# First MLP product in seven block products, token sums beside the second product, and a residual kept in DRAM

## The chip, the cores and the metric

The program runs on one core of a Trainium2 chip. The metric is the device time of one execution in microseconds (us). A core has a matrix engine (TensorE, PE in the rows; its weight loads are PEld), a vector engine (VectorE, DVE), a scalar engine (ScalarE, ACT), GpSimd (POOL) and a queue that issues transfers (SyncE, SP). Each engine takes its own instructions in order; semaphores join them. Matrix products are summed in eight PSUM banks of 128 x 512 float32; everything else lies in SBUF, with 128 partitions.

## The reference, cut to what matters

Two layers of a hybrid backbone on 640 tokens (512 latent, 128 context), model width 1024. Layer 0 mixes by a recurrence and a Fourier transform, layer 1 by attention. What the change touches is the channel mixer at the end of each layer and its modulation:

```python
def ada_params(cond, w, b):
    m = jax.nn.silu(cond) @ w + b
    return jnp.split(m[..., None, :], 6, axis=-1)
...
def mlp(h, w1, b1, w2, b2):
    return jnp.square(jax.nn.relu(h @ w1 + b1)) @ w2 + b2
...
        xs = layer_norm(ALPHA * xs + ms[2] * ys, ln1_g[layer], ln1_b[layer])
        hs = modulate(xs, ms[3], ms[4])
        xs = layer_norm(ALPHA * xs + ms[5] * mlp(hs, w1[layer], b1[layer], w2[layer], b2[layer]),
                        ln2_g[layer], ln2_b[layer])
```

The context tokens go the same way with modulation vectors of their own. `w1` is 1024 x 4096, `w2` 4096 x 1024, all in float32.

## The kernel before, in words

**Products.** Every float32 operand is held as a high part `hi` and a low part `lo` (two float32r values that sum to it), and a product is three matmuls: weight hi by token hi, weight hi by token lo, weight lo by token hi. L210 issues nearly all of them.

**Weights.** Weights stream in units of 128 x 1024. SP loads a unit into one of three `raw` slots; `pump` (L163) takes it on: ACT copies the high part (L170), DVE subtracts it for the low part (L171), both into one of four `sp` slots. Two units are kept ready ahead. A `w1` unit holds 128 of the 4096 hidden columns, over all 1024 rows.

**The MLP** (`mlp`, L1026 on) goes through the hidden columns in four quarters b. In a quarter, eight `w1` units give 48 matmuls each (three products, eight row chunks, and the 640 tokens as 384 and 256 columns), 384 in all. A unit leaves PSUM through ACT (L1020, adds the bias), DVE (L1022, squared ReLU), ACT (L294, high part) and DVE (L297, low part) into `h1`. Then eight `w2` units, four for each half n of the output columns, give 240 matmuls of 512 columns (`tok_k_outer`): five token tiles of 128 stand in five banks at once, and after the fourth unit DVE multiplies each by the gate (L490) and POOL adds it into the residual `x` in SBUF (L493). The last quarter's second product is done tile by tile with the closing layer norm (`tail`).

**The first quarter** has extra work. The layer norm before it ends there: four `w1` units run early on the tokens that are ready (EARLY), while the last tiles are transposed. Then `make_base` scales `x` and adds gate times bias: POOL L504 for two products, DVE L506 for five tiles.

**Modulation of the next layer.** While layer 0's MLP runs, DVE works out the modulation vectors of layer 1 (`ada_sum_gen`): 48 steps, each with a 512 KB weight tile from DRAM and two passes of 128 x 1024 into `acc` (L428 the first, L430 after), one step for each weight unit that `next` hands out. After eight steps PE sums over the partitions, and DVE adds the bias (L455); gates go through a small DRAM buffer (`gscr`, POOL DMA L463).

**Slots.** `R` has 6 large tiles (tokens `hT` 2, `h1` 2, `x` and others), `vec` 4, `n` 6 of 128 x 1024, `acc` 1. A tile that asks for a slot waits for its last reader. The order on each engine is the program's order as a scheduler lays it out.

## Time and profile before

| | |
|---|---|
| Median of three runs | 1516.93 us (1514.2 to 1518.15) |
| The profiled execution | 1518.29 us, span of its trace 1516.2 us |
| Mean granted TensorE clock | 0.984 |
| PE / DVE / ACT / POOL busy | 1464.1 / 850.8 / 594.4 / 286.1 us |

The span is from the first to the last instruction; 2.1 us of the execution's time lie outside it. Busy times are sums over an engine's instructions. The layer-0 MLP runs from about 249 to 711 us and the layer-1 MLP from about 1058 us to the end.

### The profile page before, as it was taken

What the parts mean: (1) busy time and instruction counts of PE and PEld (TensorE: products, weight loads), DVE (VectorE), ACT (ScalarE), POOL (GpSimd) and SP (SyncE); (2) the same over time, 40 slices, a digit from 0 to 9 for tenths busy, and PEclk for the clock granted to TensorE, in tenths of its full rate; (3) what the DMA queues carried; (4) which work ended last, traced back from release to release, by engine and by line L of the source; (5) the groups of instructions that cost most, each with busy time, mean ns of one, the idle gap of its engine ahead of it and who ended that gap; (6) DMA issues with size and microseconds to landing.
All of it is one profiled execution on the core that took longest, in us unless ns stands there. A gap on an engine that the chain in (4) does not pass through costs nothing.

```text
span 1516.2 us, 21740 instructions
## 1 busy us (share of the span) xinstructions
PE 1464.1 (97%) x8572; PEld 1266.9 (84%) x8572; DVE 850.8 (56%) x1541; ACT 594.4 (39%) x1061; POOL 286.1 (19%) x327
## 2 busy tenths in 40 slices
PE   6999899999999999999899999999999999999997
PEld 4768677888988988988688888877998998988986
DVE  6756768974864865337744455547833333323345
ACT  4557436421321321336455455646531331321331
POOL 1145103104004004002412222322202103003000
PEclk9999999999999999999899999999999999999999
DMA  9445834453643642220533131431322222222211
GB/s 384 148 164 172 306 108 146 152 194 106 196 151 112 196 147 89 84 97 30 209 106 105 60 136 60 161 109 42 127 82 77 77 78 76 74 79 84 70 56 70
DMA packets 56373, 186.60 MB, mean 123 GB/s; under 512 B 10440, under 2 KB 10824, under 8 KB 56272
## 3 DMA queue, kind: packets, MB, share of 16 engines
q1 hardware_dynamic: 55440, 184.14, 35.3%
q8 instruction: 67, 1.10, 0.3%
q0 software_dynamic: 832, 1.09, 0.2%
q14 instruction: 34, 0.28, 0.1%
HBM read 178.87 MB, written 6.33 MB: 122 GB/s over the span
## 4 chain that ended last, share of the span: by engine, by line
PE 76%; DVE 11%; ACT 5%; issue 4%; POOL 2%; DMA 2%; SPq 0%; POOLq 0%; DVEq 0%; ACTq 0%
PE bank L210 74%; DVE sp L171 2%; PE bank L1212 1%; POOL ln L514 1%; ACT R L755 1%; DVE R L506 1%; DVE R L297 1%; DVE R L495 1%; ACT junk L512 1%; DVE R L526 1%; DVE ln L533 1%; DVE acc L430 1%; ACT n L567 1%; DVE n L524 1%; POOL n L1202 1%
## 5 line engine op out<-in xcount | busy, mean ns | idle before, releaser
L210 PE MATMUL bank<-R,sp 128*128 128x384 f32 (+1 forms) x4368 | 664.5, 311 | 10.7 <-POOL R L296 3.6
L210 PEld LDWEIGHTS bank<-R,sp 128*128 128x128 f32 x4368 | 642.7, 190 | 28.4 <-issue 7.5
L210 PE MATMUL bank<-sp,R 128*128 128x512 f32 x2580 | 613.4, 396 | 7.1 <-DVE sp L171 2.6
L210 PEld LDWEIGHTS bank<-sp,R 128*128 128x128 f32 x2580 | 484.2, 189 | 128.3 <-issue 8.2
L171 DVE TENSOR_TENSOR sp<-raw,sp 128x1024 fp32r<-128x1024 f32 (+1 forms) x177 | 219.1, 1240 | 171.5 <-ACT sp L170 166.8
L170 ACT ACTIVATE sp<-raw 128x1024 fp32r<-128x1024 f32 (+1 forms) x177 | 186.1, 1056 | 316.0 <-PE bank L210 299.0
L493 POOL TENSOR_TENSOR R<-R,n 128x512 f32<-128x512 f32 x60 | 91.0, 1551 | 499.8 <-DVE n L490 499.8
L1022 DVE SCALAR_TENSOR_TENSOR n<-n 128x640 f32<-128x640 f32 x64 | 52.6, 822 | 189.3 <-ACT n L1020 189.3
L1020 ACT ACTIVATE n<-bank,pack 128x384 f32<-128x384 f32 (+1 forms) x128 | 61.2, 524 | 234.0 <-PE bank L210 228.4
L430 DVE SCALAR_TENSOR_TENSOR acc<-n,cx,acc 128x1024 f32<-128x1024 f32 x84 | 110.5, 1352 | 7.4 <-DMA n<-in_ada_w_dram 7.4
L297 DVE TENSOR_TENSOR R<-n,R 128x640 fp32r<-128x640 f32 (+2 forms) x123 | 98.6, 805 | 14.1 <-POOL R L296 11.1
L490 DVE TENSOR_TENSOR n<-bank,vec 128x512 f32<-128x512 f32 x100 | 67.3, 685 | 40.7 <-PE bank L210 36.6
L294 ACT ACTIVATE R<-n 128x640 fp32r<-128x640 f32 (+1 forms) x88 | 61.6, 704 | 44.3 <-DVE n L1022 39.5
L514 POOL TENSOR_TENSOR ln<-ln,mhalf 128x1 f32<-128x1 f32 x35 | 20.1, 575 | 296.8 <-DVE ln L513 296.8
L512 ACT ACTIVATE junk<-R,ln 128x1024 bf16<-128x1024 f32 x35 | 40.3, 1151 | 84.7 <-DVE ln L522 60.2
L210 PE MATMUL bank<-R,R 128*128 128x512 f32 x240 | 62.5, 405 | 0.0
L1202 POOL TENSOR_SCALAR n<-n,mx 128x384 f32<-128x384 f32 (+1 forms) x80 | 43.1, 541 | 91.1 <-DVE mx L1199 46.8
L567 ACT ACTIVATE n<-bank,mod 128x128 f32<-128x128 f32 x120 | 45.3, 455 | 26.5 <-PE bank L560 26.5
L210 PEld LDWEIGHTS bank<-R,R 128*128 128x128 f32 x240 | 44.4, 188 | 11.0
L1216 ACT ACTIVATE n<-bank 128x384 f32<-128x384 f32 (+1 forms) x80 | 32.9, 448 | 49.8 <-PE bank L1212 43.4
L1187 DVE CUSTOM_DVE_ANT_0 n<-bank,vec 128x256 f32<-128x256 f32 (+3 forms) x128 | 40.4, 350 | 13.2 <-PE bank L210 8.9
L1192 ACT ACTIVATE n<-n,mx 128x384 f32<-128x384 f32 x64 | 38.8, 610 | 20.4 <-DVE mx L1190 16.9
(153 smaller groups left out, 923.7 us busy)
## 6 DMA issues: line engine op xcount, KB each, us to landing
raw<-in_wts_dram SPq DMA_DIRECT2D x184, 512.0 KB, 3.2
n<-in_ada_w_dram SPq DMA_DIRECT2D x80, 512.0 KB, 4.4
vec<-in_rpb_dram SPq DMA_DIRECT2D x16, 512.0 KB, 3.9
R<-in_ada_dram SPq DMA_DIRECT2D x15, 512.0 KB, 10.0
vec<-in_vecs_dram SPq DMA_DIRECT2D x13, 512.0 KB, 5.3
vec<-gscr SPq DMA_DIRECT2D x10, 512.0 KB, 4.8
R<-in_x_dram SPq DMA_DIRECT2D x5, 512.0 KB, 5.0
R<-in_xg_dram SPq DMA_DIRECT2D x5, 512.0 KB, 5.9
```

Of the source, the lines that this page charges most:

```text
L170: self.nc.scalar.activation(s.t[:, 0, :cols], r.t[:, :cols], AF.Copy)
L171: self.nc.vector.tensor_tensor(out=s.t[:, 1, :cols], in0=r.t[:, :cols], in1=s.t[:, 0, :cols].bitcast(F32), op=OP.subtract)
L210: self.nc.tensor.matmul(out, lhsT, rhs, start=start, stop=stop)
L294: self.nc.scalar.activation(hi, src, AF.Copy)
L297: (self.nc.vector if lo_eng == "dve" else self.nc.gpsimd).tensor_tensor(out=lo, in0=src, in1=hi.bitcast(F32), op=OP.subtract)
L430: nc.vector.scalar_tensor_tensor(acc.t[:, cond, :], w.t, f, acc.t[:, cond, :], op0=OP.mult, op1=OP.add)
L490: nc.vector.tensor_tensor(out=tmp.t[:, :512], in0=o.t, in1=gates[t // 4].t[:, c], op=OP.mult)
L493: nc.gpsimd.tensor_tensor(out=x[:, t, c], in0=x[:, t, c], in1=tmp.t[:, :512], op=OP.add)
L512: nc.scalar.activation(self.junk, src, AF.Square, bias=m[:, 2:3], accum_out=m[:, 4:5])
L567: nc.scalar.activation(dst, tr.t[:, j * 128:(j + 1) * 128], AF.Identity, bias=sh, scale=sc)
L1020: nc.scalar.activation(v[:, c0:c1], o.t[:, :c1 - c0], AF.Identity, bias=b)
L1202: nc.gpsimd.tensor_scalar(p.t[:, :n], p.t[:, :n], m[:, 5:6], 1.0, op0=OP.mult, op1=OP.mult)
```

## The change

**Pairs by block products.** In quarters b = 1 to 3, two `w1` units are done together (`w1_pair`). Two units are 256 hidden columns; the 1024 rows are halved (`hT[0]`, `hT[1]`), the 640 tokens are halved, and the 256 columns are halved by unit. The 2 x 2 x 2 block product that needs eight block products is done with seven (the Winograd form of Strassen's scheme). A block product (`block_mm`) is 12 matmuls of 320 columns into one bank, so that a pair has 84 matmuls. Three of the four pieces of weight go through sums: POOL makes four sums of 128 x 512 (L209 to L212) from the two raw units, and the pair is split in four pieces (`split_pair`): one raw unit, two sums of 1024 columns, half a raw unit, by ACT L174 and DVE L175. Three pieces are kept ready ahead. The blocks leave PSUM by one ACT copy and seven DVE operations of 128 x 320 (L1164 to L1187); squared ReLU is on ACT for the first unit and on DVE (L1155) for the second; the second unit's low part is made on POOL (L355).

**Token sums.** The tokens' sums and differences of blocks (`T12`, `T34`, two more `R` tiles with hi and lo) are made once for each layer by `token_sums`, during the second product of quarter 0: eight steps, each with POOL full values (L1105, 128 x 640), a DVE sum (L1117 to L1130), an ACT high part and a DVE low part (L355). In layer 0 a step goes with each of the eight units; in layer 1 two steps with each of the last four.

**Residual in DRAM.** `x`, after its scaling, is written to DRAM (`xsum`, ten pieces of 256 KB) and its `R` slot freed. DVE multiplies a tile of the second product by its gate (L1197), and a POOL DMA with accumulation adds it to its piece in DRAM (L1199, 60 in all). In the last quarter `x` is read back.

**Order.** In layer 0, the scaling now stands ahead of the modulation work, which makes no step in the early units, two for each of the last four units of quarter 0, and 1.5 or 2 for each unit of the second products, none in the pairs. The sixth part of the modulation (the MLP gate of layer 1) is moved to layer 1's own quarter 0; there the scaling follows when its gate has come back (`late_base`, behind the fourth unit of the second product).

```diff
+    def split_pair(self, s):
+        nc = self.nc
+        r = self.raws
+        if self.sub == 0:
+            r0, r1 = r[0].t, r[1].t
...
+            self.split_unit(s, r0, 1024)
+            nc.gpsimd.tensor_tensor(out=s1, in0=r1[:, :512], in1=r1[:, 512:], op=OP.add)
+            nc.gpsimd.tensor_tensor(out=s2, in0=s1, in1=r0[:, :512], op=OP.subtract)
+            nc.gpsimd.tensor_tensor(out=s3, in0=r0[:, :512], in1=r1[:, :512], op=OP.subtract)
+            nc.gpsimd.tensor_tensor(out=s4, in0=r0[:, 512:], in1=s2, op=OP.subtract)
+            r.pop(0).done()
+        elif self.sub < 3:
+            self.split_unit(s, self.sums[self.sub - 1].t, 1024)
...
+            self.split_unit(s, r[0].t[:, 512:], 512)
...
+    def token_sums(self, hT, sums):
...
+        for g in range(2):
+            fa, a = full(0, 1, g)
+            fb, t1 = full(0, 0, g)
+            nc.vector.tensor_tensor(out=t1, in0=a, in1=t1, op=OP.subtract)
+            put(0, 0, g, t1)
+            yield
...
+    def w1_pair(self, l, m, hT, sums, dst):
...
+        s = self.next_sub()
+        o, p = self.block_mm(s, 0, hT[0], 0)
+        nc.scalar.activation(t1, p, AF.Copy)
+        o.done()
+        o, p = self.block_mm(s, 512, hT[1], 0)
+        stt(c11, p, b[0], t1, op0=OP.add, op1=OP.add)
+        o.done()
+        s.done()
+        s = self.next_sub()
+        o, p = self.block_mm(s, 512, T12, H2)
+        tt(out=u2, in0=p, in1=t1, op=OP.add)
...
+    def evac_sum(self, o, t, n, gates):
...
+        nc.vector.tensor_tensor(out=tmp.t[:, :512], in0=o.t, in1=gates[t // 4].t[:, n * 512:(n + 1) * 512], op=OP.mult)
+        o.done()
+        nc.gpsimd.dma_start(out=self.xsum[t][n], in_=tmp.t[:, :512], accum_op=OP.add)
+        tmp.done()
...
+                if l == 0:
+                    load_base()
+                    base()
+                self.ada = self.ada_sum_gen(1, range(5) if l == 0 else (5,))
+                next(self.ada)
+                self.ada_rate = ADA_W1
...
+                if self.paired(("w1", l, b * 8 + m)):
+                    self.w1_pair(l, b * 8 + m, hT, sums, [h1[(m + i) // 4].t[:, (m + i) % 4] for i in range(2)])
...
+                def late_base():
+                    self.ada_flush()
+                    base()
+                    to_memory()
+                    self.side, self.side_steps = self.token_sums(hT, sums), 2
...
-                        self.evac_gated(outs[t], x.t, t, n, gates)
+                        self.evac_sum(outs[t], t, n, gates)
```

Three places show what this makes of the engines' order. The first is DVE in layer 0 around the end of the second product of quarter 0 (`bank_135` to `bank_139` before and `bank_135` on after are the five tiles of the second column half; `acc` is the modulation's sum). Before:

```order
L171 TENSOR_TENSOR sp_40_3120<-raw_42_2986,sp_40_3120 128x1024
L171 TENSOR_TENSOR sp_41_3159<-raw_43_3040,sp_41_3159 128x1024
L171 TENSOR_TENSOR sp_42_3225<-raw_44_3084,sp_42_3225 128x1024
L490 TENSOR_TENSOR n_123_3194<-bank_135_3042,vec_10_2429 128x512
L490 TENSOR_TENSOR n_124_3197<-bank_136_3049,vec_10_2429 128x512
```

After:

```order
L355 TENSOR_TENSOR R_21_2872<-n_129_3138,R_21_2872 128x2x320
L355 TENSOR_TENSOR R_22_2940<-n_132_3206,R_22_2940 128x2x320
L511 TENSOR_TENSOR n_130_3189<-bank_140_3192,n_130_3189 128x512
L482 TENSOR_SCALAR acc_3_3198<-n_125_3085,cx_118 128x1024
L483 TENSOR_SCALAR acc_3_3198<-n_125_3085,cx_118 128x1024
L175 TENSOR_TENSOR sp_41_3208<-vec_13_3149,sp_41_3208 128x1024
L486 SCALAR_TENSOR_TENSOR acc_3_3198<-n_128_3136,cx_118,acc_3_3198 128x1024 x2
L486 SCALAR_TENSOR_TENSOR acc_3_3198<-n_131_3201,cx_118,acc_3_3198 128x1024 x2
L528 TENSOR_SCALAR mod_122<-bank_141_3241 128x4 x4
L175 TENSOR_TENSOR sp_42_3265<-vec_14_3150,sp_42_3265 128x1024
L486 SCALAR_TENSOR_TENSOR acc_3_3198<-n_133_3252,cx_118,acc_3_3198 128x1024 x2
L1197 TENSOR_TENSOR n_136_3298<-bank_135_3099,vec_10_2417 128x512
```

The five tiles' evacuations stood right behind the weight splits; now the token sums, modulation passes and splits of sums stand in front of them.

The second is DVE in a pair of layer 0's quarter 3 (`raw` a unit as loaded, `vec` a POOL sum, `n` a work tile, `bank` a block product). Before, a unit of quarter 1:

```order
L1022 SCALAR_TENSOR_TENSOR n_132_3354<-n_132_3354 128x640
L171 TENSOR_TENSOR sp_45_3429<-raw_47_3228,sp_45_3429 128x1024
L297 TENSOR_TENSOR R_21_3209<-n_132_3354,R_21_3209 128x640
L430 SCALAR_TENSOR_TENSOR acc_3_3220<-n_135_3427,cx_108,acc_3_3220 128x1024 x2
```

After, a pair of units:

```order
L175 TENSOR_TENSOR sp_92_5161<-raw_76_5000,sp_92_5161 128x1024
L1169 TENSOR_TENSOR n_199_5127<-bank_225_5172,n_198_5126 128x320
L1172 TENSOR_TENSOR n_198_5126<-bank_226_5186,n_199_5127 128x320
L175 TENSOR_TENSOR sp_93_5200<-vec_31_5162,sp_93_5200 128x1024
L1176 SCALAR_TENSOR_TENSOR n_199_5127<-bank_227_5203,pack,n_199_5127 128x320
L1178 TENSOR_TENSOR n_199_5127<-bank_226_5186,n_199_5127 128x320
L1181 SCALAR_TENSOR_TENSOR n_198_5126<-bank_228_5218,pack,n_198_5126 128x320
L175 TENSOR_TENSOR sp_94_5232<-vec_32_5163,sp_94_5232 128x1024
L1187 TENSOR_TENSOR n_199_5127<-n_199_5127,bank_229_5239 128x320
L1155 SCALAR_TENSOR_TENSOR n_199_5127<-n_199_5127 128x640
L175 TENSOR_TENSOR sp_95_5258<-raw_77_5011,sp_95_5258 128x512
L355 TENSOR_TENSOR R_27_5124<-n_198_5126,R_27_5124 128x640
```

The block operations are those of the quarter's first pair, and the splits between them those of the second; in this stretch no modulation pass is left.

The third is POOL at the end of layer 0's second product. Before, the ten additions of a quarter stand alone:

```order
L493 TENSOR_TENSOR R_15_1734<-R_15_1734,n_118_3030 128x512
L493 TENSOR_TENSOR R_15_1734<-R_15_1734,n_123_3194 128x512
L493 TENSOR_TENSOR R_15_1734<-R_15_1734,n_124_3197 128x512
L493 TENSOR_TENSOR R_15_1734<-R_15_1734,n_125_3200 128x512
L493 TENSOR_TENSOR R_15_1734<-R_15_1734,n_126_3203 128x512
```

After, of quarter 2's end and quarter 3's first pairs:

```order
L209 TENSOR_TENSOR vec_31_5162<-raw_77_5011 128x512
L210 TENSOR_TENSOR vec_31_5162<-vec_31_5162,raw_76_5000 128x512
L211 TENSOR_TENSOR vec_32_5163<-raw_76_5000,raw_77_5011 128x512
L212 TENSOR_TENSOR vec_32_5163<-raw_76_5000,vec_31_5162 128x512
L1199 DMA xsum_1_66<-n_193_5109 128x512
L1199 DMA xsum_1_68<-n_194_5112 128x512
L1199 DMA xsum_1_70<-n_195_5115 128x512
L1199 DMA xsum_1_72<-n_196_5118 128x512
L1199 DMA xsum_1_74<-n_197_5121 128x512
L209 TENSOR_TENSOR vec_33_5292<-raw_79_5170 128x512
```

The sums of the quarter's second pair (`vec_31`, `vec_32`) stand ahead of the five accumulating transfers of the second column half, those of the third pair (`vec_33`) behind them.

## Rows read from the trace of the kernel before

**Rows 1.** The page: busy time, share and count of each engine, and the chain of work that ended last, by engine and by line.

```profile
PE 1464.1 (97%) x8572; PEld 1266.9 (84%) x8572; DVE 850.8 (56%) x1541; ACT 594.4 (39%) x1061; POOL 286.1 (19%) x327
...
PE 76%; DVE 11%; ACT 5%; issue 4%; POOL 2%; DMA 2%; SPq 0%; POOLq 0%; DVEq 0%; ACTq 0%
```

**Rows 2.** The same chain in order of time, four of its pieces: start us, us, what.

```profile
287.60 1.15 DVE sp L171
288.79 35.63 PE bank L210 x224
...
553.77 127.98 PE bank L210 x698
...
1077.90 421.16 PE bank L210 x2399
```

**Rows 3.** The engines' busy time by stage (us, with counts), the granted clock, DMA share, GB/s: the first quarter's first and second product and the second quarter's first product in layer 0, the third quarter's second product there, the same of layer 1, and a later first product of layer 1.

```profile
244.00:318.00 74.00, 67.53 (x430) 64.33 (x429) 65.26 (x75) 38.35 (x68) 16.31 (x12) 0.95 0.54 182
318.00:373.00 55.00, 55.00 (x247) 44.88 (x249) 36.23 (x40) 8.30 (x10) 13.28 (x9) 1.00 0.46 153
373.00:430.00 57.00, 57.00 (x391) 56.16 (x388) 39.73 (x44) 18.96 (x29) 2.44 (x2) 1.00 0.49 157
...
1052.00:1123.00 71.00, 65.88 (x424) 63.63 (x423) 47.83 (x58) 37.56 (x67) 14.39 (x13) 0.95 0.34 115
...
1178.00:1233.00 55.00, 55.00 (x384) 54.95 (x383) 21.14 (x23) 19.44 (x30) 3.13 (x2) 1.00 0.23 77
```

**Rows 4.** PE over the second quarter of layer 1: start us, us, instruction, count.

```profile
1177.45 55.27 PE L210 MATMUL bank<-R,sp 128*128 128x384 f32 x384
1232.57 54.86 PE L210 MATMUL bank<-sp,R 128*128 128x512 f32 x240
```

**Rows 5.** Groups of instructions by line and shape: count, busy us, mean ns of one, idle time before them.

```profile
L171 DVE TENSOR_TENSOR sp<-raw,sp 128x1024 fp32r<-128x1024 f32 x176 | 217.3, 1236 | 171.5 <-ACT sp L170 166.8
L170 ACT ACTIVATE sp<-raw 128x1024 fp32r<-128x1024 f32 x176 | 185.7, 1059 | 316.0 <-PE bank L210 299.0 <-DMA raw<-in_wts_dram 16.9
...
L490 DVE TENSOR_TENSOR n<-bank,vec 128x512 f32<-128x512 f32 x100 | 67.3, 685 | 40.7 <-PE bank L210 36.6 <-POOL R L493 4.1
...
L297 DVE TENSOR_TENSOR R<-n,R 128x640 fp32r<-128x640 f32 x72 | 59.7, 829 | 2.3 <-ACT R L294 2.3
L294 ACT ACTIVATE R<-n 128x640 fp32r<-128x640 f32 x72 | 53.2, 740 | 39.8 <-DVE n L1022 39.5
L1022 DVE SCALAR_TENSOR_TENSOR n<-n 128x640 f32<-128x640 f32 x64 | 52.6, 822 | 189.3 <-ACT n L1020 189.3
...
L506 DVE SCALAR_TENSOR_TENSOR R<-R,n 128x1024 f32<-128x1024 f32 x20 | 29.9, 1532 | 0.0
...
L504 POOL TENSOR_TENSOR n<-vec,vec 128x1024 f32<-128x1024 f32 x8 | 21.7, 2720 | 26.6 <-DVE R L297 25.8 <-DVE R L1099 0.8
...
L1187 DVE CUSTOM_DVE_ANT_0 n<-bank,vec 128x320 f32<-128x320 f32 x32 | 15.4, 481 | 1.5 <-PE bank L210 1.5
...
L428 DVE TENSOR_SCALAR acc<-n,cx 128x1024 f32<-128x1024 f32 x12 | 8.8, 745 | 0.0
```

**Rows 6.** Single lines of the code: durations in ns (least, median, greatest), first and last start, shape; the modulation pass, POOL's addition and a POOL product of 640 columns.

```profile
L430 DVE SCALAR_TENSOR_TENSOR acc<-n,cx,acc x84: 1266/1277/3393, 259.8 to 575.3; 128x1024 f32<-128x1024 f32 x84
...
L493 POOL TENSOR_TENSOR R<-R,n x60: 1281/1302/2357, 342.9 to 1398.7; 128x512 f32<-128x512 f32 x60
...
L766 POOL TENSOR_TENSOR R<-R,R x8: 1557/1567/4678, 72.3 to 125.3; 128x640 f32<-128x640 f32 x8
```

**Rows 7.** POOL's five additions after each column half of layer 0's first second product, start us, us, count, idle before.

```profile
342.88 9.38 POOL L493 TENSOR_TENSOR R<-R,n 128x512 f32<-128x512 f32 x5 [69.43 <-DVE n L490]
...
369.10 6.34 POOL L493 TENSOR_TENSOR R<-R,n 128x512 f32<-128x512 f32 x5 [16.83 <-DVE n L490]
```

**Rows 8.** DVE in the same stretch, start us, us, count.

```profile
343.32 1.95 DVE L430 SCALAR_TENSOR_TENSOR acc<-n,cx,acc 128x1024 f32<-128x1024 f32 x1
345.19 0.68 DVE L490 TENSOR_TENSOR n<-bank,vec 128x512 f32<-128x512 f32 x1
345.79 1.73 DVE L430 SCALAR_TENSOR_TENSOR acc<-n,cx,acc 128x1024 f32<-128x1024 f32 x1
347.44 1.27 DVE L490 TENSOR_TENSOR n<-bank,vec 128x512 f32<-128x512 f32 x2
```

**Rows 9.** What PE waited for in the last part of layer 0's layer norm and its first units (240 to 295 us): engine, line, what for, us in total, times, longest.

```profile
PE bank L210 <- DVE sp L171: 1.4, 1, 1.4
PE bank L210 <- DVE R L297: 0.7, 1, 0.7
```

**Rows 10.** DVE at 433 to 437 us, while POOL issued four small transfers to `gscr`.

```profile
433.94 0.82 DVE L297 TENSOR_TENSOR R<-n,R 128x640 fp32r<-128x640 f32 x1
...
435.34 2.47 DVE L430 SCALAR_TENSOR_TENSOR acc<-n,cx,acc 128x1024 f32<-128x1024 f32 x2
```

**Rows 11.** POOL at the same time.

```profile
433.65 2.33 POOL L463 DMA_DIRECT2D gscr<-n  x4 [58.22 <-DVE n L455]
```

**Rows 12.** The two transfers of 256 KB that POOL issues (the `new_v` output): the issue's duration in ns, and the time from issue to landing, least, median and greatest.

```profile
L1107 POOL DMA_DIRECT2D out_new_v_dram<-R x2: 947/982/1018, 760.2 to 881.3; - x2
...
DMA to landing us min/median/max: 5.4/6.8/8.2
```

**Rows 13.** A line of the page's DMA issues: engine, count, KB each, median us to landing.

```profile
vec<-gscr SPq DMA_DIRECT2D x10, 512.0 KB, 4.8
```

More of the change, by code (lines that the diff above doesn't have):

```diff
@@ L32 @@
 MASKED = -1e30
-SPLIT_PRI = 0
 LN_ACT = 2
@@ L144, in __init__ @@
         self.xscr = dr.tile([NT, 128, D], F32, name="xscr")
+        self.xsum = [[dr.tile([128, 512], F32, name=f"xsum{t}_{n}") for n in range(2)] for t in range(NT)]
         self.plan = stream_plan()
@@ L161, in psum @@
         return self.bank.get(shape or [128, 512])
[L164 to L173 removed]
+    @staticmethod
@@ new lines, in paired, with split_unit @@
+    def paired(key):
+        return key[0] == "w1" and key[2] >= PLAIN
+    def split_unit(self, s, src, cols):
+        self.nc.scalar.activation(s.t[:, 0, :cols], src[:, :cols], AF.Copy)
+        self.nc.vector.tensor_tensor(out=s.t[:, 1, :cols], in0=src[:, :cols],
+                                     in1=s.t[:, 0, :cols].bitcast(F32), op=OP.subtract)
+    def pump(self):
+        while self.raws:
+            key = self.plan[self.split_pos] if self.split_pos < len(self.plan) else None
+            pair = self.paired(key)
+            if len(self.ready) >= (3 if pair else self.AHEAD) or not (self.sp.free or self.extra):
+                break
+            if pair and self.sub == 0 and len(self.raws) < 2:
+                break
+            s = self.sp.get([128, 2, 1024], F32R) if self.sp.free else self.extra.pop(0)
+            if pair:
+                self.split_pair(s)
+            else:
+                r = self.raws.pop(0)
+                cols = 384 if key == ("dft", 2) else 1024
+                self.split_unit(s, r.t, cols)
+                r.done()
+                self.split_pos += 1
@@ L179, in add_extra, with next_sub @@
+    def next_sub(self):
+        if not self.ready:
+            self.pump()
+        s = self.ready.pop(0)
+        self.pump()
+        return s
     def add_extra(self):
@@ L197, in next @@
         self.seen += 1
-        if self.ada_every and self.seen % self.ada_every == 0:
-            next(self.ada, None)
+        self.ada_due += self.ada_rate
+        while self.ada_due >= 1.0:
+            self.ada_due -= 1.0
+            if next(self.ada, None):
+                break
+        for _ in range(self.side_steps if self.side is not None else 0):
+            next(self.side, None)
         assert self.plan[self.pos] == key, (self.plan[self.pos], key)
@@ L475, in ada_sum_finish, with ada_flush @@
         ab.done()
-        if p == 5:
-            self.ada_done |= {(l, 1), (l, 2)}
-    def ada_flush(self, l):
-        while not {(l, 1), (l, 2)} <= self.ada_done:
-            next(self.ada, None)
+    def ada_flush(self):
+        for _ in self.ada:
+            pass
     def evac_gated(self, o, x, t, n, gates, sums=None):
@@ L1075, in mlp @@
                 r.done()
-        return new, pend
+        return new, pend, x
     KEY0 = (0, 64, 192, 256)
```

210 lines of the change are left out of this document (160 added, 50 removed).

## The prediction

> **What bounds the kernel now.** I read the page first: PE is busy 97% of the span, and the chain that ended last is PE for 76%, nearly all of it L210 [rows 1]. A mean says little about one stage, so the chain in order of time comes next: one piece of PE, 421.16 us and 2399 matmuls long, covers layer 1's MLP from its first units to the last tiles, and 127.98 us without a break stand at the end of layer 0's [rows 2]. The stage table agrees: PE is busy for the whole of each middle stretch at a granted clock of 1.00, while DVE has 36 to 40 us of work in 55 to 57 in layer 0 and 21 of 55 in layer 1, and POOL 2 to 13 [rows 3]. So the middle quarters are bound by the number of PE columns alone, a matmul taken out is worth its full time, and the other engines have room that the change spends. The beginnings of the MLPs differ: DVE is busy 65.26 of 74 us there in layer 0, and PE loses time at a clock of 0.95 [rows 3].
>
> **Matmuls removed.** A `w1` quarter takes 55.27 us for 384 matmuls, 0.1439 us for a mean of 320 columns [rows 4]. A block product has matmuls of 320 columns, 84 for a pair where two units had 96: 12.09 us for 13.82. Four pairs lose 48 matmuls, 6.91 us; six quarters (three in each layer) 41.4 us. This is the whole gain; the rest asks how much comes back.
>
> **What a pair costs the others.** DVE: 3.5 splits of 1.24, one squared ReLU of 0.82, one low part of 0.83, and seven operations of 320 columns with one input in PSUM at 0.48 (the nearest row, L1187, is another operation of that shape) [rows 5], in all 9.4 us. POOL: four sums of 1.30 and a low part of 1.56 [rows 6], 6.8 us. ACT: 3.5 copies of 1.06, four passes of 0.74 [rows 5] and the copy of a block, about 7.2 us. Each is below 12.09. But DVE and POOL hinder each other: five additions take 9.38 us beside modulation passes and 6.34 without, and in the same stretch passes of 1.28 became 1.95 and 1.73, while L490, with one input in PSUM, stayed at 0.68 [rows 6 to 8]. I read this as exclusion between POOL and DVE operations with two SBUF inputs. Then 4.33 + 0.82 + 0.83 + 6.8 = 12.7 us of a pair exclude each other, just over PE's 12.09. What saves it is the order: POOL's sums for a quarter's first two pairs stand before the transfers that close the second product, so four pairs leave 4 x 7.5 + 2 x 5.2 = 41 us inside 48.4, and the second product takes the other 10 us beside 10 us of splits, of 55. So PE stays the bound; for waits at pair ends, where a split stands behind an evacuation on DVE, I take 2 us over six quarters (0 to 8).
>
> **Layer 0, quarter 0, second product.** This is the worst place. Between the last unit's evacuation and the first tile of the second column half, DVE now has 8 splits (9.9 us), 16 token-sum operations of 640 columns (13.3), 20 modulation passes at 1.28 (25.5) and four at 0.75, five gate products at 0.69, and some 4 us of small work and the last unit's remainder [rows 5, 6]: 59 us. POOL has eight full values of 1.57 and eight sums of 1.30 [rows 6], 23 us; half of it at least stands ahead of the same point. Before, DVE had 36.23 in 55 [rows 3]. PE finishes the first tile of the second half about 49 us into the product (the last unit's five tiles take 6.9) and the product at 54.9 [rows 4]. If POOL's work lay wholly beside DVE's idle and one-input work, DVE would come to that tile at about 58; if all excludes, at 59 + 15 = 74. PE has three banks free, so it can run three block products, to 55 + 5.2 = 60. Between the ends, at 66, it stands still for 6 us, and about 3 more are lost while the five evacuations and a split queue in front of the pair's own: +9, bounds 0 and 74 - 60 + 3 = +17, rounded to 18.
>
> **Layer 0, later quarters.** The second product of quarter 1 holds 16 modulation steps, 32 passes or 41 us, 10 of splits, 7 of gate products and 10 of POOL sums: 68 if all exclude, 58 if not, against 55. Eight of the passes stand inside the following pairs. I take +2.5 (0 to 8).
>
> **Layer 1, quarter 0.** The gate now comes late: modulation sum, POOL issue, DRAM, back at 4.8 us [rows 13], two POOL products of 2.72 and five scalings of 1.53 [rows 5]. It stands behind the fourth unit, so about 25 us into the second product. Then 16 token-sum operations (13.3), POOL's eight values (12.5), five gate products (3.4) and four splits (5) follow, 34 us if they exclude, done at 59 to 63, and the pair's third block asks for `T12` at 55 + 2 x 1.73 = 58.4. I take +5; bounds 0, if the values overlap, and +15, if the gate's way is 10 us longer.
>
> **Starts.** In layer 0 the scaling precedes the modulation; PE waited 1.4 us for a split and 0.7 for a low part there [rows 9], and the last split in the chain stands at 287.60 [rows 2]. I take -1.5 (-2.1 to 0). In layer 1, 16 passes are new beside the last four units, with DVE busy 47.83 of 71 [rows 3]: they fit on average, one queued before a split costs up to 1.3, so +1.5 (0 to 4).
>
> **Accumulating transfers.** No row shows one. Instead of POOL's 1.30 a tile costs an issue; the nearest is the plain store of 256 KB, issue 0.98, landing 5.4 to 8.2 [rows 12]. The five tiles hold five of the six `n` slots until landing; the pair's second work tile waits for the first of them. That tile is done 4 us before the product's end and is needed 5 us after it, so a landing up to 10 us is covered. I cost it at 0, bounds 0 and +10 (landing 11.7 in six quarters). The read-back can start when the last pair's first block is done, six blocks (10.4 us) before the product's end, and the first tile needs it two units (2 x 6.9 us) into the next product: 24 us for ten pieces, so 0. The Trainium skill, "DMA: Bandwidth & Descriptors", Anatomy of one DMA (SWDGE path), gives about 2.0 us and the bytes at 436 GB/s, here 2.6 us (an estimate from that page); the row's 5.4 is twice that, so the row decides, and by either the term stays 0.
>
> **Sum.** -41.4 + 2 + 9 + 2.5 + 5 - 1.5 + 1.5 + 0 = -22.9 against the profiled 1518.29: 1495.4. The median before is 1.4 below that execution, so the forecast is 1494 us.
>
> **Rivals.**
> - *All is hidden.* The stretches in which DVE and POOL collide stay under PE's time, as in the trace, where 36 us of DVE and 13 of POOL made no gap in PE. Then only -41.4 stands: 1516.9 - 41.4 = 1475.5. For it: most of what POOL does now comes while DVE waits for PE. Against it: DVE's 59 us in 55 exceed PE even alone.
> - *Overload at the upper bounds.* 18 + 8 + 15 and 4 at the layer-1 start come back: -41.4 + 45 + 2 - 1.5 = +4, and about -1 with one of them not full: 1516. It speaks for it that POOL's passes can stretch beyond the sum of both: one took 2.36 for 1.30, one pass of DVE 3.39 for 1.28 [rows 6].
> - *Slower: the accumulation lands late.* It must read, add and write. From 10 us on, each further us in landing holds the pair's second work tile, and with it DVE's queue and the splits behind it, once in each of six quarters: 6 x (landing - 10). It eats the 23 us at 14; at 16 us, three stores' least time, it is +36, so 1494 + 36 = 1530. Against it: a landing has to be 2.4 times the stored 6.8. A rule would bring this about in another way: POOL could be hindered in writing descriptors while DVE works. Here four issues took 2.33 us in all with DVE at passes and low parts throughout, and those stayed at 2.47 for two and 0.82 [rows 10, 11]; so a share of this case's chance only. The rule is the Trainium skill's, "SBUF — State Buffer", box "The DVE blocks DMA trap (SWDGE)" under its section on the two sides of SBUF: DVE in its two-port modes locks out the descriptor writer. The trace has no delay of that kind.
> - *It doesn't do what it says.* The matmuls taken out are plain in the program's order (288 fewer), so only a clock below 1.00 in thinner PE work could undo it: at 0.95 over the six quarters' 290 us, +15.
>
> **How the numbers follow.** A measurement here tells about 0.3%, 4.6 us, from no change. Forecast with its neighbours 0.52 (own range 1482 to 1508), all hidden 0.22 (1474 to 1480), overload 0.12 (1509 to 1522), late landing 0.11 (over 1521 for 0.09 of it), the last 0.03. Faster than 1512.4 has 0.52 + 0.22 + 0.05 = 0.79; between that and 1521.5 0.06 of the overload, and 0.03 of late landing and the last, 0.09; slower 0.12. For 8 in 10 the range goes from 1475 to 1514.
>
> **What would show it.** Right: 84 matmuls of 320 columns for each pair 0.144 us apart, 48.4 us for a paired quarter; a gap or slow blocks in PE at the end of quarter 0's second product in layer 0 of 5 to 15 us, with PE waiting for banks that L1197 frees, and a smaller one in layer 1 with PE waiting for the low parts of L355; L209 to L212 above 1.30 in the mean; L1199 landing in 5 to 10 us. Wrong: PE gaps in every pair (exclusion decides, and no quarter is near 48.4), no gap at quarter 0 (all hidden), or waits on `n` behind L1199 (late landing).

## The result, and the profile after

The changed kernel takes 1524.55 us (median of 5 runs, 1523.33 to 1529.0) where the kernel before took 1515.61: a ratio of 1.0066, 95% interval 1.0044 to 1.0088. It is slower, by 9 us; the forecast was 1494, with a range of 1475 to 1514. The profiled span is 1522.1 us.

The page of the changed kernel, busy time of each engine and the DMA issues that are new in kind:

```profile
PE 1435.8 (94%) x8284; PEld 1228.4 (81%) x8284; DVE 1033.2 (68%) x1741; ACT 640.2 (42%) x1101; POOL 487.3 (32%) x463
...
xsum<-n POOLq DMA_DIRECT2D x60, 256.0 KB, 5.9
```

Beside [rows 1], PE has the 288 matmuls less and 28 us less to do, DVE 182 us more and POOL 201 more. The time didn't follow PE, so PE must wait. Here is what it waited for over the whole span, the four longest: engine, line, releaser, us in total, times, longest.

```profile
PE bank L266 <- DVE sp L175: 21.8, 14, 3.4
PE bank L266 <- DVE acc L486: 11.9, 3, 7.1
PE bank L686 <- ACT n L598: 9.6, 1, 9.6
PE bank L266 <- DVE R L355: 8.0, 6, 4.7
```

L686 is the program's start. PE waits far longer for the splits (L175) than before, when it was 4.5 us, and the modulation passes (L486) are new in this list. Where they fall is read from the stage table of the changed kernel: in layer 0 the second product of quarter 0, then quarter 1's and quarter 2's first and second products and quarter 3's first; in layer 1 the second product of quarter 0 and the first ones of quarters 1 and 2 (columns as in [rows 3]).

```profile
309.00:382.00 73.00, 63.74 (x266) 48.44 (x259) 65.46 (x62) 15.76 (x20) 30.33 (x18) 0.93 0.55 158
382.00:445.00 63.00, 53.70 (x337) 52.12 (x337) 59.12 (x70) 23.90 (x33) 30.42 (x18) 0.95 0.49 142
445.00:514.00 69.00, 61.65 (x263) 46.60 (x262) 47.01 (x46) 10.99 (x13) 22.87 (x17) 0.93 0.58 167
514.00:572.00 58.00, 51.83 (x335) 50.32 (x334) 54.51 (x60) 23.48 (x32) 27.73 (x18) 0.97 0.43 120
572.00:629.00 57.00, 57.00 (x256) 45.93 (x256) 22.96 (x30) 11.10 (x12) 18.60 (x18) 1.00 0.42 108
629.00:678.00 49.00, 49.00 (x337) 49.00 (x336) 42.32 (x50) 24.81 (x33) 23.19 (x14) 1.00 0.57 162
...
1138.00:1198.00 60.00, 57.19 (x246) 46.19 (x241) 43.66 (x36) 14.13 (x18) 32.25 (x23) 0.97 0.47 137
1198.00:1250.00 52.00, 50.17 (x340) 49.56 (x339) 46.68 (x53) 24.80 (x33) 30.70 (x20) 1.00 0.40 106
1305.00:1354.00 49.00, 49.00 (x336) 49.00 (x335) 42.37 (x50) 24.89 (x33) 23.15 (x14) 1.00 0.44 123
```

Four stretches of layer 0 lose, and there the granted clock is below 1.00 too; the last quarter of layer 0 and the later ones of layer 1 run as the matmul count says. Stage by stage, from the start of one product to the start of the next (us, from PE's timeline of both traces; the last column is the kernel before, less the 6.9 us that the prediction takes off a paired quarter):

| layer 0 | before | after | by the matmul count |
|---|---|---|---|
| second product, quarter 0 | 56.6 | 72.1 | 56.6 |
| first, quarter 1 | 58.1 | 63.0 | 51.2 |
| second, quarter 1 | 56.1 | 68.9 | 56.1 |
| first, quarter 2 | 58.1 | 58.5 | 51.2 |
| second, quarter 2 | 56.6 | 56.6 | 56.6 |
| first, quarter 3 | 56.6 | 49.2 | 49.7 |

From the MLP's first product to the end of quarter 3's first, layer 0 goes from 410.0 to 432.6 us, +22.6; layer 1, to the end of its last matmul, from 448.8 to 436.8, -12.0; the stretches outside shrank by 4.7. The sum is the span's +5.9. So layer 1 came out near the forecast and layer 0 did the opposite. Of the 4.7, 3.8 lie ahead of layer 0's MLP, which the traces of all fourteen kernels start anywhere from 245.7 to 252.1 us; so that part isn't a gain of the change.

PE in the two second products that lose, start us, us, count, idle before:

```profile
318.53 34.76 PE L266 MATMUL bank<-sp,R 128*128 128x512 f32 x150
353.22 1.05 PE L266 MATMUL bank<-acc,ones 128*32 128x512 f32 x4
358.77 1.92 PE L266 MATMUL bank<-acc,ones 128*32 128x512 f32 x4 [4.50 <-DVE acc L486]
360.62 8.75 PE L266 MATMUL bank<-sp,R 128*128 128x512 f32 x30
372.86 0.66 PE L524 MATMUL bank<-ident,n 128*128 128x128 f32 x4 [3.49 <-DVE n L511]
373.27 8.71 PE L266 MATMUL bank<-sp,R 128*128 128x512 f32 x30
...
494.52 1.92 PE L266 MATMUL bank<-acc,ones 128*32 128x512 f32 x4 [7.07 <-DVE acc L486]
```

PE meets DVE's lateness first at the modulation's own partition sums, which stand in the middle of its queue, and 30 matmuls behind such a gap take 8.75 us where 150 ahead of it took 34.76 (6.95 for 30): that is the clock. It is granted at 0.93 in the mean over this product, between full speed (2.4 GHz) and the lower level (1.2 GHz); it was 1.00 before the gaps, as in [rows 3], and 0.81 in the stretch with them (columns as in [rows 3]):

```profile
330.00:355.00 25.00, 24.27 (x106) 18.69 (x104) 20.55 (x22) 3.38 (x4) 7.19 (x7) 1.00 0.82 210
355.00:382.00 27.00, 19.73 (x70) 14.33 (x71) 26.41 (x19) 5.79 (x7) 17.05 (x9) 0.81 0.38 120
```

DVE is busy for 26.41 of the 27 us with the gaps.

### The profile page after: what moved, and what is told of

Same layout as the page of the kernel before. It is cut to its first block, busy times and chain, and to the rows that moved or that the text cites. A ratio compares the mean times of both kernels' runs of the same rounds, so it can differ in the third digit from the quotient of the medians.

```text
span 1522.1 us, 21897 instructions
## 1 busy us (share of the span) xinstructions
PE 1435.8 (94%) x8284; PEld 1228.4 (81%) x8284; DVE 1033.2 (68%) x1741; ACT 640.2 (42%) x1101; POOL 487.3 (32%) x463
## 5 line engine op out<-in xcount | busy, mean ns | idle before, releaser
L266 PE MATMUL bank<-R,sp 128*128 128x320 f32 (+3 forms) x4080 | 628.4, 313 | 27.9 <-DVE sp L175 17.2
L266 PEld LDWEIGHTS bank<-R,sp 128*128 128x128 f32 x4080 | 604.0, 190 | 47.8 <-DVE sp L175 20.6
L266 PEld LDWEIGHTS bank<-sp,R 128*128 128x128 f32 x2580 | 485.3, 190 | 135.7 <-issue 12.8
L175 DVE TENSOR_TENSOR sp<-raw,sp 128x1024 fp32r<-128x1024 f32 (+2 forms) x177 | 243.3, 1377 | 95.2 <-ACT sp L174 93.8
L174 ACT ACTIVATE sp<-raw 128x1024 fp32r<-128x1024 f32 (+2 forms) x177 | 174.9, 995 | 234.1 <-PE bank L266 204.4
L486 DVE SCALAR_TENSOR_TENSOR acc<-n,cx,acc 128x1024 f32<-128x1024 f32 x84 | 119.0, 1444 | 16.4 <-DMA n<-in_ada_w_dram 16.3
L355 DVE TENSOR_TENSOR R<-n,R 128x640 fp32r<-128x640 f32 (+2 forms) x115 | 110.6, 966 | 13.6 <-POOL R L354 9.7
L174 ACT ACTIVATE sp<-vec 128x1024 fp32r<-128x1024 f32 x48 | 49.8, 1054 | 107.9 <-PE bank L266 89.5
L175 DVE TENSOR_TENSOR sp<-vec,sp 128x1024 fp32r<-128x1024 f32 x48 | 63.0, 1314 | 37.8 <-ACT sp L174 37.7
L355 POOL TENSOR_TENSOR R<-n,R 128x640 fp32r<-128x640 f32 x24 | 49.5, 2060 | 111.2 <-ACT R L352 111.2
L209 POOL TENSOR_TENSOR vec<-raw 128x512 f32<-128x512 f32 x24 | 40.1, 1672 | 137.5 <-DMA raw<-in_wts_dram 83.1
L1199 POOL DMA_DIRECT2D xsum<-n x60 | 55.1, 1215 | 90.5 <-DVE n L1197 90.1
L266 PE MATMUL bank<-R,R 128*128 128x512 f32 x240 | 62.6, 406 | 0.0
L1197 DVE TENSOR_TENSOR n<-bank,vec 128x512 f32<-128x512 f32 x60 | 39.4, 685 | 21.2 <-PE bank L266 13.1
L266 PEld LDWEIGHTS bank<-R,R 128*128 128x128 f32 x240 | 44.4, 188 | 11.1
```

The costliest lines, as they stand in the source:

```text
L174: self.nc.scalar.activation(s.t[:, 0, :cols], src[:, :cols], AF.Copy)
L175: self.nc.vector.tensor_tensor(out=s.t[:, 1, :cols], in0=src[:, :cols], in1=s.t[:, 0, :cols].bitcast(F32), op=OP.subtract)
L209: nc.gpsimd.tensor_tensor(out=s1, in0=r1[:, :512], in1=r1[:, 512:], op=OP.add)
L266: self.nc.tensor.matmul(out, lhsT, rhs, start=start, stop=stop)
L355: (self.nc.vector if lo_eng == "dve" else self.nc.gpsimd).tensor_tensor(out=lo, in0=src, in1=hi.bitcast(F32), op=OP.subtract)
L486: nc.vector.scalar_tensor_tensor(acc.t[:, cond, :], w.t, f[cond], acc.t[:, cond, :], op0=OP.mult, op1=OP.add)
```

## The experiments

Twelve runs, each beside the kernel before on the same chip. The letters are the theories that the expectations name: M, the modulation passes overload DVE; A and S, accumulating transfers hold the work tiles; T, the token sums decide; Q, PE's small products stand in the way; P, what is moved is lost at its new place; X, POOL and DVE exclude each other in the pairs; B, the passes carried into a pair decide by themselves. The table has the four stretches of layer 0 that lose, in us from start to start; the ratio is to the kernel before, with its interval.

| run | 2nd, q0 | 1st, q1 | 2nd, q1 | 1st, q2 | median | ratio |
|---|---|---|---|---|---|---|
| the change | 72.1 | 63.0 | 68.9 | 58.5 | 1524.6 | 1.0066 (1.0044 to 1.0088) |
| e1 no passes | 72.5 | 49.3 | 57.8 | 49.3 | 1494.6 | 0.9863 (0.9832 to 0.9893) |
| e2 cheap tokens | 57.2 | 61.7 | 68.1 | 58.6 | 1512.9 | 0.9979 (0.9963 to 0.9994) |
| e3 free sums | 60.8 | 82.2 | 58.8 | 60.7 | 1523.7 | 1.0055 (1.0032 to 1.0078) |
| e4 pairs in layer 1 | 64.8 | (58.1) | 56.2 | (58.1) | 1506.2 | 0.9937 (0.9917 to 0.9957) |
| e6 shared tiles | 70.5 | 59.7 | 59.9 | 59.2 | 1506.1 | 0.9943 (0.9925 to 0.9962) |
| e9 rates | 56.6 | 64.2 | 64.6 | 49.9 | 1532.5 | 1.0122 (1.0103 to 1.0140) |
| e10 rates, tiles | 56.6 | 57.2 | 56.6 | 49.3 | 1505.5 | 0.9938 (0.9915 to 0.9960) |
| e5 two quarters | 57.1 | (57.8) | 55.0 | 55.8 | 1489.9 | 0.9841 (0.9819 to 0.9863) |
| e12 no passes, tiles | 70.3 | 49.3 | 57.8 | 49.3 | 1484.1 | 0.9791 (0.9762 to 0.9821) |
| e13 no weight sums | 65.7 | 51.9 | 60.1 | 49.2 | 1485.0 | 0.9797 (0.9775 to 0.9818) |
| e11 two quarters, tiles | 58.5 | (57.8) | 55.0 | 52.4 | 1485.7 | 0.9796 (0.9779 to 0.9814) |
| e14 spread | 55.9 | 55.8 | 61.7 | 56.1 | 1509.6 | 0.9958 (0.9943 to 0.9973) |

In brackets: quarters that are not paired there.

**e1, no modulation passes.**

```diff
-            else:
+            elif len(parts) != 5:
                 for cond in range(2):
                     nc.vector.scalar_tensor_tensor(acc.t[:, cond, :], w.t, f[cond], acc.t[:, cond, :],
...
```

> Leaves out 35 of the 40 modulation steps' DVE work in layer 0's MLP (of each part only the first of eight row chunks is summed, so layer 1's modulation is wrong); transfers, PE's partition sums and all else stay. Theory M (the modulation work, packed into 20 units beside token sums, overloads DVE in layer 0): the four stretches of layer 0 that are over the forecast (second products of quarters 0 and 1, first products of quarters 1 and 2, about 52 us together above what the matmul count gives) fall to under 12, the time to 1478 to 1486 us. Theory T (token sums, or the exclusion of POOL and DVE in the pairs, decide) and theory A (accumulating transfers hold the work tiles): little comes back, 1508 us or more.

Three of the four stretches fall by 13.7, 11.1 and 9.2 us, 34 together: the passes decide there. The first doesn't move, and the time came out some 9 us above M's range for that reason. That speaks less against M than it seems. In this kernel nothing reads most of the modulation's weight tiles, and SP's queue stood in that stretch until they had landed:

```profile
SPq L468 <- DMA n<-in_ada_w_dram: 49.0, 16, 7.6
```

The weights of the pairs, POOL's sums and the token sums came late behind it, and PE waited 13.9 us at the modulation's transposes (L524), as in e12 below. So e1 decides nothing about the first stretch; e2 and e9 do.

**e2, cheap token sums.**

```diff
-                    self.side, self.side_steps = self.token_sums(hT, sums), 1
+                    self.side, self.side_steps = self.token_sums(hT, sums, True), 1
...
```

> Layer 0's token sums lose their POOL values and all their DVE operations: each of the eight steps only copies high parts by ACT, so the block products of layer 0 have wrong tokens. Modulation stays. Theory M: DVE loses 13 us and POOL 13 us of work in the second product of quarter 0, so that stretch and the pairs behind it give back 10 to 20 us, the second product of quarter 1 (about 69 us) and the pairs behind it stay as they are: 1505 to 1515 us. Theory T: 35 to 50 us come back, 1475 to 1490 us. Theory A: the work tiles that token sums held are free, so 5 to 10 us, 1514 to 1519 us.

The mirror image: 15 us go in the first stretch, and the other three stay. The time, 12 us shorter, lies in M's 10 to 20, though the pairs behind, which M had giving back too, moved by 1.3 only. In that stretch 22 passes (the four first ones among them) cost next to nothing without token sums.

**e3, PE never waits for DVE's modulation sums.**

```diff
-                self.mm(bank.t[g * 32:(g + 1) * 32, :], self.ones, acc.t[:, cond, hf * 512:(hf + 1) * 512], True, True)
+                self.mm(bank.t[g * 32:(g + 1) * 32, :], self.ones, (acc.t[:, cond, :] if p == 5 or l == 0 else self.fake)[:, hf * 512:(hf + 1) * 512], True, True)
...
-                nc.tensor.transpose(tr.t[:, j * 128:(j + 1) * 128], row[:, j * 128:(j + 1) * 128], self.ident)
+                nc.tensor.transpose(tr.t[:, j * 128:(j + 1) * 128], (row if l == 0 else self.fake)[:, j * 128:(j + 1) * 128], self.ident)
...
```

> PE's small products and transposes for layer 1's modulation (parts 0 to 4) read a tile that has long been there instead of the sums that DVE makes, so that PE never waits for DVE at these places; DVE's work is all there, layer 1's modulation is wrong. Theory Q (PE stands because these products lie in its queue in the middle of the second products): the waits of 4.5, 3.5 and 7.1 us go for good, and the lower clock behind them, so 1498 to 1506 us. Theory M: DVE is as late as before and PE meets it at the next evacuation or split, so 1514 to 1524 us, with longer gaps behind the second products.

The gaps in the second products go (60.8 and 58.8), and quarter 1's pairs take 82.2 instead of 63.0; the four stretches together take 262.5 us in both kernels. Theory Q falls: where PE first meets DVE's lateness is not what it costs.

**e4, pairs in layer 1 alone.**

```diff
-        return key[0] == "w1" and key[2] >= PLAIN
+        return key[0] == "w1" and key[1] == 1 and key[2] >= PLAIN
...
-                self.ada_rate = ADA_W2[l][b]
+                self.ada_rate = 1.0 if l == 0 else ADA_W2[l][b]
...
```

> Layer 0's MLP without pairs and token sums, modulation at one step for each unit through its units as before the change (the early units excepted); residual in DRAM and accumulating transfers in both layers; layer 1 as changed. Theory M: layer 0 is as long as before the change, and layer 1 keeps the 12 us that it gained: 1500 to 1506 us. Theory A: layer 0's middle quarters get longer by the accumulating transfers alone, with gaps in PE, 1510 us or more.

9 us faster than before: layer 1 gains 12.3 us, and layer 0 loses 4.9, since its first second product takes 64.8 us for 56.6. There DVE waited for the modulation's bias tile, and SP's queue, before it issued that load, for a work tile that a modulation pass still read:

```profile
DVE n L511 <- DMA n<-in_ada_b_dram: 9.4, 1, 9.4
...
SPq L502 <- DVE acc L483: 7.1, 1, 7.1
```

DVE's evacuations, which stand ahead of that pass, had waited 1.6 us for an accumulating transfer; that much is A's. The load then took some 10 us to land, and whether the five accumulating transfers issued in the 7 us before it had a part in that isn't shown: in the kernel before, too, DVE waited for this tile, 11.1 us at two places.

**e6, two gate products to a work tile.**

```diff
-        tmp = self.n.get([128, 1024])
+        if t % 2 == 0:
+            self.two = self.n.get([128, 1024])
+        v = self.two.t[:, t % 2 * 512:t % 2 * 512 + 512]
...
```

> The changed kernel, but two gate products of a column half share one work tile of 1024 columns, so that five accumulating transfers hold three of the six tiles and not five. Theory S (the 16 us that quarter 0's second product of layer 0 still loses without modulation passes come from work tiles held by the accumulating transfers, and from SP's and POOL's queues behind whoever waits for one): that stretch falls from 72 to 58 to 66 us, the time to 1510 to 1519 us. Theory T (it is the token sums' own work on DVE and POOL): 1521 us or more.

The gain is larger than S had it (18 us against the change), and the place was wrong: quarter 1's second product falls from 68.9 to 59.9, layer 1's quarter 0 from 59.7 to 55.8, quarter 1's pairs by 3; the stretch I meant hardly moves. What happened in quarter 1's second product of the changed kernel: DVE, with the idle time before each,

```profile
476.46 0.69 DVE L1197 TENSOR_TENSOR n<-bank,vec 128x512 f32<-128x512 f32 x1 [2.07 <-DMA xsum<-n]
...
480.65 1.22 DVE L175 TENSOR_TENSOR sp<-raw,sp 128x1024 fp32r<-128x1024 f32 x1
490.79 5.88 DVE L486 SCALAR_TENSOR_TENSOR acc<-n,cx,acc 128x1024 f32<-128x1024 f32 x4 [8.92 <-DMA n<-in_ada_w_dram]
```

and what SP's queue waited for in the same stretch, with the releaser:

```profile
SPq L502 <- DMA xsum<-n: 7.0, 1, 7.0
```

Five accumulating transfers hold five of six work tiles. SP stood 7.0 us at the modulation's bias load for want of a tile, the weight loads behind it went out at 479.5 us and landed at 490.8, and DVE idled for 8.92 us in a stretch that was thought too full of DVE's work. With shared tiles that wait on `xsum` is gone, as what DVE and SP waited for in this stretch of e6 shows:

```profile
DVE acc L486 <- DMA n<-in_ada_w_dram: 5.9, 6, 1.9
...
SPq L502 <- DMA gscr<-n: 0.4, 1, 0.4
```

Layer 1 shows it too: the second product of its quarter 0 takes 55.6 to 56.3 us in all six kernels with shared tiles and 58.2 to 62.6 in the seven without (54.7 before the change), and the pairs behind it fall from 51.6 to 49.2 in e6.

**e9 and e10, other rates, without and with the shared tiles.**

```diff
-ADA_W2 = ((1.5, 2.0, 2.0), (2.0, 0.0, 0.0))
+ADA_W2 = ((0.25, 1.5, 1.5), (2.0, 0.0, 0.0))
```

> The changed kernel with another table of rates: modulation steps for each unit of layer 0's second products 0.25, 1.5, 1.5 instead of 1.5, 2, 2; what is left (about 8 of 40 steps) stands in one piece at the start of the last quarter's second product. Theory M (passes beyond what a second product has room for, about 29 us of 55): the pairs of quarters 1 and 2 come to 49 to 52 us each, the second product of quarter 1 to 56 to 61, that of quarter 0 to 58 to 64; the piece at the end costs 3 to 15: 1488 to 1500 us. Rival P (the number of passes is the same, so what is moved is lost at its new place): 1510 us or more.

> The rates of the run before and the shared work tiles together. Theories M and S: 0 to 5 us faster than with the rates alone, since few modulation loads are left beside the token sums. If S is wrong: the same within 2 us.

e9 is slower still. The first stretch is at 56.6, with six modulation passes in it where the change has 22, and token sums and unshared tiles as they were; so there it is the passes that are too many. But quarter 1's pairs stay at 64.2, where M had 49 to 52; eight passes still stand at their head, 12.69 us of DVE, and PE waited 6.1 us behind them. Quarter 2's second product now takes 67.4, quarter 3's pairs 58.5, and the piece at the end some 16 us. With the tiles e10 is 27 us faster than e9, far over the forecast 0 to 5, and equal to e6: what was moved is paid at its new place. Rival P was right.

**e12, no passes and shared tiles.** The edits of e1 and e6.

> Shared work tiles, and 35 of the 40 modulation steps' DVE work in layer 0's MLP left out (so layer 1's modulation is wrong). Without the passes alone, quarter 0's second product in layer 0 stayed at 72.7 us, with the tiles alone at 70.7. Theory M and S, two limits of like size over each other there (DVE's passes; work tiles held by transfers): with both gone it comes to 56 to 61 us and the time to 1478 to 1484 us. Rival T (the token sums' chain from POOL over DVE and ACT and back is the limit by itself): it stays above 66 us, 1487 to 1495 us.

The first stretch stays at 70.3, above the rival's 66, so my reading of it as those two limits one over the other isn't borne out. In this run SP's queue waited 48.2 us there for earlier modulation weights to land (nothing reads them now), POOL 9.1 us at its first weight sum for a raw unit behind them, the token sums behind that, and PE 10.9 us at L524. The time is near what M and S had only because the later stretches are as in e1. That chain is partly made by the edit, so the run says little of the changed kernel's own 15 us.

**e13, no weight sums in layer 0.**

```diff
+            if self.plan[self.split_pos][1] == 0:
+                r.pop(0).done()
+                self.sub = 1
+                return
             nc.gpsimd.tensor_tensor(out=s1, in0=r1[:, :512], in1=r1[:, 512:], op=OP.add)
...
```

> Shared work tiles, and in layer 0 POOL's four weight sums of each pair are left out (the pieces are split from a raw unit in their place, so the block products are wrong); passes, token sums and all splits stay. With the tiles alone the pairs of quarters 1 and 2 took 59.9 and 59.3 us, against 49.4 where DVE comes without a backlog. Theory X (in a pair POOL's sums and DVE's splits exclude each other so far that a backlog can't be worked off): both quarters come to 50 to 54 us, the time from 1506 to 1488 to 1496 us. Rival B (the backlog's passes themselves stand before the pair's splits, whatever POOL does): 57 to 60 us each, 1500 to 1505 us.

Quarters 1 and 2 come to 51.9 and 49.2 against e6's 59.7 and 59.2: X holds, and the gain against e6, 21 us, is 3 more than its range allowed. The passes are still there. The same row for the modulation passes in quarter 1's pairs, in the change, in e6 and in e13: us of the stretch, DVE busy with that line alone (count), clock, DMA share, GB/s.

```profile
382.00:445.00 63.00, 15.78 (x11) 0.95 0.49 142
```

```profile
383.00:443.00 60.00, 16.62 (x11) 0.97 0.52 148
```

```profile
378.00:430.00 52.00, 12.59 (x11) 1.00 0.58 165
```

Eleven passes, which DVE's order carries over from the second product into the pairs, cost 2.7 us where POOL is free (51.9 against 49.2 undisturbed), and some 10 us where POOL makes its sums. The edit also takes away what the splits could wait for, sums that come late. But DVE hardly waited in either run (1.8 us in e6, 2.0 in e13); it was busy almost throughout, and for 8 us less with nearly as many operations, as the rows of all engines show, e6 first (columns as in [rows 3]):

```profile
383.00:443.00 60.00, 52.49 (x338) 50.83 (x337) 57.89 (x69) 24.33 (x32) 31.55 (x18) 0.97 0.52 148
```

```profile
378.00:430.00 52.00, 50.10 (x338) 49.30 (x337) 49.66 (x67) 23.71 (x32) 10.17 (x8) 1.00 0.58 165
```

What the exclusion looks like where both have work, in a pair of quarter 1 of the changed kernel, DVE first and POOL below it (start us, us):

```profile
406.70 1.91 DVE L355 TENSOR_TENSOR R<-n,R 128x640 fp32r<-128x640 f32 x1
408.54 1.90 DVE L1155 SCALAR_TENSOR_TENSOR n<-n 128x640 f32<-128x640 f32 x1
410.36 1.76 DVE L175 TENSOR_TENSOR sp<-raw,sp 128x512 fp32r<-128x512 f32 x1
```

```profile
405.77 2.16 POOL L210 TENSOR_TENSOR vec<-vec,raw 128x512 f32<-128x512 f32 x1
407.89 1.87 POOL L211 TENSOR_TENSOR vec<-raw,raw 128x512 f32<-128x512 f32 x1
409.72 1.85 POOL L212 TENSOR_TENSOR vec<-raw,vec 128x512 f32<-128x512 f32 x1
```

Each takes nearly as long as both together, as if they took turns: 0.82 (the first two of DVE's rows, alone) becomes 1.9, and 1.30 becomes 1.85 to 2.16.

**e5 and e11, two paired quarters in layer 0,** token sums in quarter 1's second product; e11 with shared tiles.

```diff
-        return key[0] == "w1" and key[2] >= PLAIN
+        return key[0] == "w1" and key[2] >= (16, 8)[key[1]]
...
-ADA_W2 = ((1.5, 2.0, 2.0), (2.0, 0.0, 0.0))
+ADA_W2 = ((1.25, 0.5, 1.25), (2.0, 0.0, 0.0))
...
-                if b == 0 and l == 0:
+                if b == 1 and l == 0:
                     self.side, self.side_steps = self.token_sums(hT, sums), 1
...
-                self.ada_rate = 0.0
-                if b == 0:
+                self.ada_rate = 1.0 if (l, b) == (0, 0) else 0.0
+                if b == 1 - l:
...
```

> In layer 0 only the last two quarters in pairs, token sums in the second product of quarter 1, modulation at 1.25 steps for each unit of the second products of quarters 0 and 2, 1 in quarter 1's first product and 0.5 in its second; layer 1 as changed. Theory M: layer 0 gains 2 x 6.9 us and layer 1 its 12: 1488 to 1496 us. Theory S: the second product with the token sums is 5 to 15 us longer: 1495 to 1505 us.

> Two paired quarters in layer 0 as in the run before, and shared work tiles. The tiles gave 4 us in layer 1's quarter 0; in layer 0 little is left for them. Theory S: 1483 to 1487 us. If the tiles only matter beside 12 or more modulation steps: 1488 to 1491 us.

Both came out as forecast, e5 by M and e11 by S: modulation has an unpaired quarter to stand in, and each second product has either token sums or many passes. e11, at 0.9796, beats both kernels by some 31 and 39 us.

**e14, three quarters with modulation spread.**

```diff
-ADA_W1 = 2.0
-ADA_W2 = ((1.5, 2.0, 2.0), (2.0, 0.0, 0.0))
+ADA_W1 = 3.0
+ADA_W2 = ((0.5, 1.5, 1.25), (2.0, 0.0, 0.0))
...
```

> Three paired quarters in layer 0, shared work tiles, and modulation where the traces show room: three steps for each of the last four units of quarter 0's first product, then 0.5, 1.5 and 1.25 for each unit of the second products; a few steps stay for the piece at the start of the last one. Theory M and X (a stretch loses what its passes, token sums, splits and POOL's sums go over it, and a pair can take up no backlog): first product of quarter 0 63 to 67 us, second product 57 to 60, pairs of quarters 1 and 2 50 to 53 each, second product of quarter 1 56 to 59: 1484 to 1492 us. If modulation costs the same wherever it stands in layer 0's MLP: 1502 to 1508 us, as with the tiles alone.

A miss, 18 us above the range; the rival, that modulation costs the same wherever it stands, is nearer, with e6, e10 and e14 within 4 us. Quarter 0's first product takes 75.0 us from start to start (the change: 64.0), the pairs 55.8 and 56.1, the last second product some 12 us more. Three steps for a unit of 6.9 us are 7.7 us of passes alone, and with a split, a squared ReLU and a low part DVE is over PE there; I had cost it at a few us. Quarter 1's pairs, though, have no modulation pass in them at all, and still take 55.8: there DVE waited for the pair's second work tile, which an accumulating transfer held although the tiles are shared.

```profile
DVE n L1169 <- DMA xsum<-n: 8.6, 1, 8.6
```

None of the three arrangements of 40 steps beside three paired quarters that ran with shared tiles (e6, e10, e14) fits layer 0; that no other does isn't shown.

## Why the prediction was wrong, point by point

By the terms of the sum, layer 0 was forecast at -9.7 us (-20.7 + 1 + 9 + 2.5 - 1.5) and came to +22.6; layer 1 at -13.2 and came to -12.0. Of layer 0's 32 us, some 28 are the later quarters, 31.4 us over the count where 2.5 and 1 of pair ends were taken.

- *Matmuls removed, -41.4.* Right in kind, a sixth too large. A paired quarter that nothing disturbs:

```profile
1304.62 49.39 PE L266 MATMUL bank<-R,sp 128*128 128x320 f32 x336
```

  That is 0.1470 us for a matmul of 320 columns, not the mean 0.1439 of [rows 4], so 49.4 for 48.4 and, against the 55.27 of [rows 4], -35.3 for six quarters.
- *What a pair costs the others.* The 41 us inside 48.4 was a fair sum of a pair's own work, and PE did stay the bound in quarters with nothing else. POOL's operations are dearer than taken: L355 2.06 us and L209 to L212 1.67 to 1.90 in the mean, for 1.56 and 1.30.
- *Layer 0, later quarters, +2.5 (0 to 8).* **This step failed first.** The text itself said that eight passes stand inside the following pairs, and I didn't add them to the pairs' 41 us. Eleven and ten passes, 15.8 and 14.2 us of DVE, on 41 us are 57 and 55 where PE needs 49: measured 63.0 and 58.5. e1 (passes out) and e13 (POOL's sums out) each take both quarters to 52 or less. Quarter 1's first product, 11.8 over the count, had no term but the 3 us of queued evacuations. Quarter 1's second product, forecast at 55 to 68 us, took 68.9, but 9 of its 12.8 us over the count came from the next step.
- *Accumulating transfers, 0.* **This step failed too.** The landing was as taken (5.9 us in the median), and the pair's second tile was waited for once, 4.3 us. But I followed the held tiles to the next pair alone, and not to the modulation's loads, which take the same tiles through SP's queue. e6 prices it: 18 us in all, 9 of them in quarter 1's second product and 6 in layer 1's quarter 0 and the pairs behind it.
- *Layer 0, quarter 0, second product, +9 (0 to 18).* Measured +15.5, inside its bounds and near the upper one: DVE came to the first tile of the second half 77 us after the product's start, where I had 58 to 74. The forecast waits for banks were, instead, PE's waits at the modulation's sums. The passes without token sums fit there (e2), and so do the token sums with 6 passes (e9) or, with shared tiles, 12 (e14); with 22 they don't. How the 15 us divide between DVE's time and its waits for POOL and transfers stays open, since e1 and e12 were no clean tests.
- *Layer 1, -20.7 with +5, +1.5 and 1 of pair ends.* -13.2 forecast, -12.0 measured, and that so near is luck. The pairs gave back 15.2 us net of their ends, where 19.7 was forecast; the start cost nothing. Quarter 0's second product cost 5.0 as taken, but not by the gate's late return: with shared tiles it costs about 1, so the other 4 us are held tiles, which were at 0.
- *Starts, -1.5 and +1.5.* The first products got shorter in both layers, by 3.8 us in layer 0 and 2.2 in layer 1, outside both ranges and to the good. PE's wait at the last transposes of the layer norm, 2.6 and 2.5 us before, is 0.65 in each; why it shrank wasn't tried.
- *The rivals.* Overload at the upper bounds is what came, beyond its price of 1516, because its terms left the pairs and the tiles out. Late landing is not: the accumulation lands like the plain store of [rows 12]. Its mechanism, a tile held until landing and a queue standing behind it, was the right one, in the main at another place than forecast. A clock that falls in thinner PE work isn't seen either: a paired quarter without waits runs at 1.00, and only stretches in which PE waits are below it.

## What to carry to other kernels

When work is moved out of some stages, sum each remaining stage again with all that the engine's order carries into it, spill from the stage ahead included; a paired quarter in which DVE is busy for 42 of 49 us has no room for 14 to 16 us of passes. For a tile held longer, list everyone who asks for a tile of that pool, and the in-order queue in which each asker stands. A gap seen at one place (here PE's small products) is only where the lateness is met: take that wait away first, as e3 did, before building on it. And an experiment that takes out an engine's work should leave the readers of its transfers, or a queue comes to wait for the landing itself, as in e1 and e12.
